# A gated DeltaNet layer with memory cross-attention on one core: side transfers issued by GpSimd, query norms from transposes, output transposes with a shorter gathering time

## The chip, the core and the metric

The kernel runs on one core of a Trainium2 chip. A core has TensorE (PE, the matrix products), VectorE (DVE), ScalarE (ACT), GpSimd (POOL) and SyncE (SP), each with an instruction queue of its own that is worked off in order, and 16 DMA engines that move data between HBM and the on-chip memory SBUF. TensorE writes its results to PSUM, a memory of eight banks, from which VectorE and ScalarE read them. An engine or a queue waits for another through semaphores. The metric is the device time of one execution in microseconds; the time before is 857.72 (median of three runs, 856.27 to 858.84).

## The reference

One layer of a hybrid decoder on 256 tokens of width 2048, all in float32. One wide projection of the normalised input gives all parts; a gated delta rule with 24 value heads (12 query/key heads, two value heads each) and a 4-head softmax cross-attention into 256 memory tokens run side by side; both are gated by SiLU and go through one output projection. Cut to what matters:

```python
h    = rms_norm(x, norm_g)
proj = einsum("bsd,de->bse", h, dn_w_in)                   # 2048 -> 11312 columns
q, k, v, a, b, xq, z = columns of proj
q, k, v = silu(causal_depthwise_conv(q, k, v, width=4))
q = l2_norm(q) * 128**-0.5 ;  k = l2_norm(k)               # per head of 128
g = -exp(a_log) * softplus(a + dt_bias) ;  beta = sigmoid(b)
# S_t = exp(g_t) S_{t-1} (I - beta_t k_t k_t^T) + beta_t v_t k_t^T ;  o_t = S_t q_t
o   = gated_delta_rule(q, k, v, g, beta)                   # chunked, by a triangular solve
mix = rms_norm(o, out_g)                                   # per head of 128
xa  = cross_attention(rms_norm(xq), rms_norm(mem) @ w_kv)  # 4 heads, 256 memory tokens
out = x + (concat(mix, xa) * silu(z)) @ w_out
```

The query's norm is a factor per token and head in front of `o`. Since `o` is normalised afterwards, the kernel doesn't divide the queries: it only needs the sum of the squares of each query, which enters the small constant inside the norm of `o`.

## The kernel before, in words

The weights lie in HBM in tiles of 128 x 1024 and are streamed through SBUF once, in the order of the list `PLAN` (lines 55 to 59): memory values and keys (V, K), gate columns (ab), cross-attention queries (x), keys and queries (k, q), values (v), gates (z), and at the end the output projection (o0 to o3). SP issues every weight load into one of five `st` buffers. For each tile ScalarE makes a rounded copy `hi` (line 342) and VectorE the rest `lo` (line 346) into one of four `wt` buffers; the products are then done as hi·hi + hi·lo + lo·hi with the same split of the activations, which gives float32 accuracy. `proj_a` (lines 362 to 376) makes transposed results (128 features by 256 tokens, PSUM `pa`), `proj_b` (lines 401 to 438) results with tokens in the partitions (`pb`).

Beside this stream run small processes, Python generators, whose instructions are strewn into it: `conv`, `gram` (products of keys, per group of two key heads), `inverse` and `merge` (the triangular inverses of 24 heads in two halves, on VectorE by 32 x 32 blocks, then on TensorE), `v_done` (the convolution of the values: shifted copies made by DMA, taps in `vw`), `delta` (the rule itself, for each of six groups of two key heads and four value heads), `split_y` (transposes of the gated outputs and their split into hi and lo), and `attend` for the cross-attention.

The order is written out by a clock of the program's own. `now` counts the estimated time of TensorE; `ve`, `se` and `po` are the engines' estimated ends; `fin` is the latest estimated end of what the current step has issued. A bare `yield` puts a process to sleep until `fin`. `yield "pe", gather` puts it into a list of those that want TensorE; when the earliest deadline (`now` + gather) is over, all in the list go on together (`step_side`, lines 221 to 228). `pe_soon(GATHER)` is a wait for `fin` plus 1.0 and then such a gathering of 0.5. `until(spare(tag))` waits, by the same clock, for a free PSUM bank; the banks are `pa` 3, `m` 2, `A` 2, `B` 1. `calm` waits until VectorE's estimated backlog is small. None of these waits exists on the chip: there, only the order of instructions and the semaphores of data and buffers count. Up to an estimated time of 45 the order is pinned; behind that, the scheduler of the language may still shift instructions within an engine.

The places that the change touches:

- `Transfers` (lines 128 to 135). `sd.dma_start` raises `fin` by 3.0 and issues from SP. It serves the gates (lines 699, 700, 703), the taps (1173), `gram` (938: two transfers of the Gram matrices to HBM per group), `inverse` (963: two loads `inN`; 989: six loads `n`; 998 and 1000: stores `dY` and `dX`; 1007: four loads into `Y`; 1010: six loads into `XN`; then a wait `LAND` of 9.0 and `merge`) and `v_done` (1182 to 1185: shifted copies `vc`; 1198: four loads `vw`; then a wait `VLAND` of 5.0). The rows of the decay (`erow`, line 734), the weights, the tokens and the results are issued with `sy.dma_start`, SP's own.
- GpSimd otherwise makes the inverse square roots, as a power −0.5 (`rsqrt`, line 270), and memsets.
- `delta` (lines 1243 to 1362). In order: products of keys and queries (`pkq`), `U` of the first block (`pU`, lines 1273 to 1275), its scaled copies, the products across the blocks, `U` of the second block, then the squares of the queries on ScalarE (lines 1324 to 1326, tile `q2` of 2 x 256), then the last products `pO` and, into a bank `m`, the sums of the squares as products with a column of ones (`pqs`, lines 1332 to 1334). Then follow the squares of `o` with an accumulated sum (line 1347), the power `e` on GpSimd and the gating.
- `split_y` (lines 1123 to 1149): for eight pairs of heads it waits for the gated outputs, then `yield "pe", GATHER_Y` with 4.0, then two banks `m`, eight transposes (`pyT`), and the split `yhi`, `ylo`, which the output projection reads.

Of the kernel before, what the change touches and what calls it, by code (L numbers as in the profile page):

```python
# [10 lines left out]
AF = mybir.ActivationFunctionType  # L11
ALU = mybir.AluOpType
# [9 lines left out]
NB = 2  # L22
C = 128
EPS = 1e-6
# [9 lines left out]
LOOK = 2  # L34
WARM = 9
GATHER = 0.5
GATHER_Y = 4.0
XPACE = 3.0
HOP = 0.25
PINNED = 45.0  # L40
# [32 lines left out]
def hybrid_kernel(ctx: ExitStack, tc: tile.TileContext, x, xT, memT, W, prm_d, cst_d, out):  # L73
    nc = tc.nc
    now, fin = [0.0], [0.0]

    def pin(ins):

        return tc.keep_in_program_order(ins) if PINNED is None or now[0] < PINNED else ins
# [8 lines left out]
    te, sy = Pinned(nc.tensor), Pinned(nc.sync)  # L88
# [17 lines left out]
    def width(ap):  # L106
        n = 1
        for d in ap.shape[1:]:
            n *= d
        return n  # L110
# [14 lines left out]
    ve, se = Engine(nc.vector, ve_cost), Engine(nc.scalar, se_cost)  # L125
    po = Engine(nc.gpsimd, lambda e, op, a, k: 0.6)

    class Transfers:


        def dma_start(self, *a, **k):
            fin[0] = max(fin[0], now[0] + 3.0)
            return sy.dma_start(*a, **k)

    sd = Transfers()

# [8 lines left out]
    def S2(name, shape, dt=F32):  # L145
        return s2p.tile([128] + list(shape), dt, name=name, tag="s2")

    def SM(name, shape, bufs=3, dt=F32):
        n = 1
        for d in shape:  # L150
            n *= d
        if n > 128:
            return smp.tile([128] + list(shape), dt, name=name, tag="s1k", bufs=6)
        if n > 16:
            return smp.tile([128] + list(shape), dt, name=name, tag="s512", bufs=3)
        return smp.tile([128] + list(shape), dt, name=name, tag=name, bufs=bufs)

    PB = {"pa": 3, "m": 2, "A": 2, "B": 1}

# [4 lines left out]
    def PS(tag, name):  # L164
        idle[tag].remove(min(idle[tag]))
        pt = ps.tile([128, 512], F32, name=name, tag=tag, bufs=PB[tag])
        held[id(pt)] = (tag, pt)
        return pt

    def spare(tag, n=1):  # L170
        return sum(t <= now[0] for t in idle[tag]) >= n

    def give(pt, t):

        idle[held.pop(id(pt))[0]].append(t)

    def bank(tag, name):
        yield from until(lambda: spare(tag))
        return PS(tag, name)

    def banks(name):
        yield from until(lambda: spare("m", 2))
        return [PS("m", name) for _ in range(2)]
# [10 lines left out]
    def mm(o_, lhsT, rhs, start, stop):  # L194
        n = width(rhs)
        if rhs.dtype == F32:
            now[0] += {32: 0.015, 64: 0.038}.get(rhs.shape[0], max(0.19, 4 * n / 2400.0))
        else:
            now[0] += max(0.092, n / 2400.0 + 0.0137) + 0.01 * (n == 256)
        te.matmul(o_, lhsT, rhs, start=start, stop=stop)  # L200

    def tr(o_, i_):
        now[0] += 0.093
        te.transpose(o_, i_, ident)
# [25 lines left out]
    def until(cond):  # L230
        while not cond():
            yield POLL

    def pe_soon(gather=0.0):

        yield max(fin[0] - now[0], 0.0) + SLACK
        yield "pe", gather
# [9 lines left out]
    def calm(queued=CALM):  # L247

        while ve.end > now[0] + queued:
            yield ve.end - now[0] - queued  # L250
# [5 lines left out]
    ones = cst[:, K_ONE : K_ONE + 1]  # L256
# [144 lines left out]
    def proj_b(steps, act, tag, done, before=None):  # L401
# [4 lines left out]
        for s in range(0, n, 2):  # L406
# [6 lines left out]
            if s == 0 or s + 2 == n:  # L413
                rk.sort()
            if s == 0 and before and tag == "A":

# [463 lines left out]
    KQ = [None] * NPAIR  # L880
# [242 lines left out]
    def split_y():  # L1123
        for j0 in (12, 14, 0, 2, 4, 6, 8, 10):
            jj = (j0, j0 + 1)
            yield from until(lambda: all(yf[j] is not None for j in jj))
            yield from calm(0.8)
            yield "pe", GATHER_Y
            pts = yield from banks("pyT")
# [45 lines left out]
    def v_done(g):  # L1175
# [13 lines left out]
        def done(r, pt):  # L1189
            def go():  # L1190
# [41 lines left out]
                if r == 1:  # L1232
                    vss[g] = raw
                    yield from delta(g)
# [8 lines left out]
    def delta(g):  # L1243

        pp = (2 * g, 2 * g + 1)
# [24 lines left out]
            ve.tensor_tensor(out=kcl[:, i], in0=pkv[i][:, 0:4:2, :], in1=kch[:, i], op=ALU.subtract)  # L1270
            give(pks[i], ve.end)
        yield from pe_soon(GATHER)
        A = yield from bank("A", "pU")
        for w, i, h in heads:
            mm(A[:, w * C : (w + 1) * C], Y[pp[i]][:, 0, h, :], vs[0][:, w, :], start=True, stop=True)
        yield 0.2
        u0s, u0 = S2("u0s", [4, C]), S2("u0", [4, C])
        ve.tensor_tensor(out=u0s, in0=A.rearrange("j (h e) -> j h e", h=4),
                         in1=ekd[:, h4].unsqueeze(2).to_broadcast([128, 4, C]), op=ALU.mult)
        se.copy(u0.rearrange("j h e -> j (h e)"), A)  # L1280
        give(A, max(ve.end, se.end))
        yield
        uh, ul = S2("uh", [4 * C], F32R), S2("ul", [4 * C], F32R)
        u0f = u0s.rearrange("j h e -> j (h e)")
        se.copy(uh, u0f)
        for i, p in enumerate(pp):
            ve.tensor_tensor(out=aT[i], in0=km[:, i].unsqueeze(2).to_broadcast([128, NB, 2, C]), in1=dT[p], op=ALU.mult)
        yield
# [3 lines left out]
        A, B = PS("A", "pU"), PS("B", "pO")  # L1292
# [19 lines left out]
        A, B = PS("A", "pU"), PS("A", "pO")  # L1312
# [8 lines left out]
        for w in range(4):  # L1321
            se.activation(oq[:, w, :], B[:, w * C : (w + 1) * C], AF.Copy, scale=egc[:, 4 * g + w : 4 * g + w + 1])
        give(B, se.end)
        q2 = S2("q2", [2, 256])
        for i, p in enumerate(pp):
            se.activation(q2[:, i, :], KQ[p][:, 1, :], AF.Square)
        yield from pe_soon(GATHER)
        yield from until(lambda: spare("B") and spare("m"))
        B, pq = PS("B", "pO"), PS("m", "pqs")
        for w, i, h in heads:  # L1330
            mm(B[:, w * C : (w + 1) * C], aT[i][:, 1, h, :], u1[:, w, :], start=True, stop=True)
        for b in range(NB):
            for i in range(2):
                mm(pq[:, 2 * b + i : 2 * b + i + 1], q2[:, i, b * C : (b + 1) * C], ones, start=True, stop=True)
        yield 0.2
        ve.tensor_tensor(out=o[1], in0=B.rearrange("c (h e) -> c h e", h=4), in1=oq, op=ALU.add)
        give(B, ve.end)

        eq, e4 = SM("eq", [4], 2), SM("e4", [3, NB, 4], 2)
        ve.tensor_scalar(out=eq, in0=pq[:, 0:4], scalar1=EPS, scalar2=EPS * 128, op0=ALU.add, op1=ALU.mult)  # L1340
        give(pq, ve.end)
        ready.add(f"d{g}")
        yield
        for b in range(NB):
            for w in range(4):
                junk = SM("ojunk", [C])
# [161 lines left out]
```

## Time and profile before

| what | value |
|---|---|
| median of 3 runs | 857.72 us (856.27 to 858.84) |
| the profiled execution | 857.04 us, of which the span of its instructions 855.3 us |
| granted TensorE clock | 1.00 |
| HBM read, written | 167.58 MB, 6.89 MB (204 GB/s over the span) |
| packets of SP's DMA queue | 145080, 180.47 MB |
| DMA issues from GpSimd | none |

A profile has one line per group of instructions: line of the code, engine, operation, the tiles as out<-in, shapes, count; then the time in which at least one of them ran, the mean length of one in ns, and the idle time of the engine before them with what ended it. The lines L86 and L103 are helpers that record every instruction, so groups are told apart by their tiles. Records of TensorE overlap, because products are pipelined and their ends are modelled: the distance from start to start says what a product costs. A float32 product that is not split makes two records, a transpose one.

### The profile page before, as it was taken

The numbers are of one execution on the slowest core, as the hardware profiler recorded it, in microseconds if no ns is written. First come the engines' busy times: TensorE is split into PE (matmuls) and PEld (weight loads), VectorE is DVE, ScalarE is ACT, GpSimd is POOL, SyncE is SP. The second block draws the span as 40 slices with busy tenths as digits, with TensorE's granted clock in tenths as the row PEclk, the third lists the DMA queues.
The fourth block names the chain that finished last, engine by engine and source line by source line (L and its number), as shares of the span: only waits on it lengthen the run. The fifth ranks groups of instructions, "written<-read, shape, count | busy, mean of one in ns | idle before, by whom it ended". The sixth has DMA issues, their size and how long they took to land.

```text
span 855.3 us, 13175 instructions
## 1 busy us (share of the span) xinstructions
PE 848.0 (99%) x4790; PEld 709.7 (83%) x4790; DVE 618.1 (72%) x1080; ACT 538.1 (63%) x929; POOL 46.5 (5%) x45
## 2 busy tenths in 40 slices
PE   9999999999999999999999999999999999999998
PEld 6888888888888888888888888788888888888886
DVE  6878886657779974788889989568886655454442
ACT  7656665798644765995966676679775654333331
POOL 1000000000000000001100202000010000000000
PEclk9999999999999999999999999999999999999999
DMA  9965566448677886869877769686755547666650
GB/s 344 335 218 177 171 189 165 146 147 263 197 208 241 263 243 180 261 210 266 226 243 218 227 214 279 198 242 222 227 158 169 186 142 265 214 210 205 199 197 25
DMA packets 145433, 181.59 MB, mean 212 GB/s; under 512 B 24824, under 2 KB 115824, under 8 KB 145368
## 3 DMA queue, kind: packets, MB, share of 16 engines
q1 hardware_dynamic: 145080, 180.47, 67.0%
q8 instruction: 37, 0.61, 0.3%
q10 hardware_dynamic: 288, 0.28, 0.1%
q14 instruction: 28, 0.23, 0.1%
HBM read 167.58 MB, written 6.89 MB: 204 GB/s over the span
## 4 chain that ended last, share of the span: by engine, by line
PE 95%; ACT 2%; DMA 1%; DVE 1%; issue 1%; SPq 0%; DVEq 0%
PE pb L86 72%; PE pa L86 13%; PE pO L86 2%; PE pU L86 2%; PE pm L86 1%; PE pkq L86 1%; PE pyT L86 1%; ACT dec L103 1%; DVE wt L346 1%; PE pqs L86 1%; PE pkk L86 1%; DMA erow<-dgc 0%; DMA st<-W_d 0%; ACT L103 0%; PE pab L86 0%
## 5 line engine op out<-in xcount | busy, mean ns | idle before, releaser
L346 DVE TENSOR_TENSOR wt<-st,wt 128x1024 fp32r<-128x1024 f32 (+1 forms) x275 | 331.9, 1212 | 164.9 <-ACT wt L342 161.2
L342 ACT CAST wt<-st 128x1024 fp32r<-128x1024 f32 (+1 forms) x275 | 286.3, 1045 | 224.3 <-PE pb L86 180.6
L86 PE MATMUL pb<-wt,hkt 128*128 128x512 f32 x1536 | 361.8, 392 | 0.0
L86 PEld LDWEIGHTS pb<-wt,hkt 128*128 128x128 f32 x1536 | 284.7, 188 | 58.7 <-DVE wt L346 0.4
L86 PE MATMUL pb<-wt,yhi 128*128 128x512 f32 x512 | 158.0, 390 | 0.0
L86 PE MATMUL pa<-hkt,wt 128*128 128x512 f32 (+1 forms) x768 | 142.8, 342 | 0.4 <-DVE wt L346 0.3
L86 PEld LDWEIGHTS pa<-hkt,wt 128*128 128x128 f32 x768 | 117.9, 188 | 18.3 <-DVE wt L346 1.0
L86 PEld LDWEIGHTS pb<-wt,yhi 128*128 128x128 f32 x512 | 95.7, 188 | 19.6
L86 PE MATMUL pb<-wt,ylo 128*128 128x512 f32 x256 | 99.7, 389 | 0.0
L86 PE MATMUL pb<-wt,mkt 128*128 128x512 f32 x384 | 88.6, 391 | 0.9 <-ACT wt L342 0.9
L86 PEld LDWEIGHTS pb<-wt,mkt 128*128 128x128 f32 x384 | 71.6, 188 | 16.8 <-ACT wt L342 1.8
L86 PEld LDWEIGHTS pb<-wt,ylo 128*128 128x128 f32 x256 | 48.1, 188 | 10.1
L103 ACT ACT_TABLE_LOAD x31 | 39.8, 1283 | 1.4 <-DVE acc L103 1.0
L103 DVE SCALAR_TENSOR_TENSOR acc<-raw,prm,acc 128x255 f32<-128x255 f32 (+2 forms) x72 | 34.2, 476 | 3.6 <-ACT acc L103 3.2
L103 DVE TENSOR_TENSOR inT<-inXT,inN 96x1 f32<-96x1 f32 (+22 forms) x92 | 29.1, 342 | 3.2 <-DMA inN<-dN 2.4
L103 DVE TENSOR_REDUCE inXT<-inT 96x1 f32<-96x1 f32 (+22 forms) x92 | 28.6, 337 | 0.7
L103 POOL TENSOR_TENSOR e<-e,mhalf 128x8 f32<-128x8 f32 x6 | 20.8, 3472 | 120.5 <-DVE e L103 120.5
L103 DVE TENSOR_TENSOR vc<-vc 128x512 f32<-128x512 f32 x36 | 24.5, 682 | 0.1
L103 POOL TENSOR_TENSOR srk<-skt,mhalf 128x4 f32<-128x4 f32 x6 | 7.0, 1175 | 224.6 <-DVE skt L103 145.6
L103 DVE SCALAR_TENSOR_TENSOR o<-o,e,zs 128x128 f32<-128x128 f32 x48 | 14.0, 345 | 7.0 <-POOL e L103 7.0
L103 ACT ACTIVATE ojunk<-o 128x128 f32<-128x128 f32 x48 | 14.4, 301 | 7.0 <-DVE o L103 4.9
L103 DVE TENSOR_TENSOR vc<-vc,vw 128x512 f32<-128x512 f32 x24 | 16.4, 683 | 2.8 <-DMA vc<-vs 2.8
(202 smaller groups left out, 693.9 us busy)
## 6 DMA issues: line engine op xcount, KB each, us to landing
st<-W_d SPq DMA_DIRECT2D x271, 512.0 KB
erow<-dgc SPq DMA_DIRECT2D x24, 256.0 KB
vw<-dtap SPq DMA_DIRECT2D x24, 256.0 KB
dN<-dec SPq DMA_DIRECT2D x12, 256.0 KB
n<-dN SPq DMA_DIRECT2D x12, 256.0 KB
vc<-vs SPq DMA_DIRECT2D x12, 224.0 KB
vc<-vc SPq DMA_DIRECT2D x12, 224.0 KB
xraw<-xT_d SPq DMA_DIRECT2D x8, 256.0 KB
```

Of the source, the lines that this page charges most:

```text
L86: return lambda *a, **k: pin(getattr(self.eng, op)(*a, **k))
L103: return pin(getattr(self.eng, op)(*a, **k))
L342: pin(se.eng.copy(hi[:, w] if parts > 1 else hi, st[:, w] if parts > 1 else src))
L346: pin(ve.eng.tensor_tensor(out=lo[:, w] if parts > 1 else lo, in0=st[:, w] if parts > 1 else src, in1=hi[:, w] if parts > 1 else hi, op=AL ...
```

## The change

Three things:

1. `sd.dma_start` issues from GpSimd's queue, no longer from SP's. What raises `fin` stays.
2. In `delta`, the four products with a column of ones go, and so do the two squares of 128 x 256 in front of them. In their place, behind the first `pU` products, four transposes bring the queries to the form tokens by features in a bank `m` (`pqT`), and four squares of 128 x 128 on ScalarE, each with an accumulated sum, give `q2` (128 x 4) directly in SBUF. The wait for a spare bank `m` moves with them.
3. `GATHER_Y` goes from 4.0 to 0.5.

```diff
-GATHER_Y = 4.0
+GATHER_Y = 0.5
...
         def dma_start(self, *a, **k):
             fin[0] = max(fin[0], now[0] + 3.0)
-            return sy.dma_start(*a, **k)
+            return pin(nc.gpsimd.dma_start(*a, **k))
...
         yield from pe_soon(GATHER)
-        A = yield from bank("A", "pU")
+        yield from until(lambda: spare("A") and spare("m"))
+        A, pq = PS("A", "pU"), PS("m", "pqT")
         for w, i, h in heads:
             mm(A[:, w * C : (w + 1) * C], Y[pp[i]][:, 0, h, :], vs[0][:, w, :], start=True, stop=True)
+        for w in range(4):
+
+            tr(pq[:, w * C : (w + 1) * C], KQ[pp[w % 2]][:, 1, w // 2 * C : (w // 2 + 1) * C])
         yield 0.2
...
         se.copy(uh, u0f)
+        q2 = SM("q2", [4], 2)
+        for w in range(4):
+            junk = SM("ojunk", [C])
+            se.activation(junk, pq[:, w * C : (w + 1) * C], AF.Square, accum_out=q2[:, w : w + 1])
+        give(pq, se.end)
...
-        q2 = S2("q2", [2, 256])
-        for i, p in enumerate(pp):
-            se.activation(q2[:, i, :], KQ[p][:, 1, :], AF.Square)
         yield from pe_soon(GATHER)
-        yield from until(lambda: spare("B") and spare("m"))
-        B, pq = PS("B", "pO"), PS("m", "pqs")
+        yield from until(lambda: spare("B"))
+        B = PS("B", "pO")
         for w, i, h in heads:
             mm(B[:, w * C : (w + 1) * C], aT[i][:, 1, h, :], u1[:, w, :], start=True, stop=True)
-        for b in range(NB):
-            for i in range(2):
-                mm(pq[:, 2 * b + i : 2 * b + i + 1], q2[:, i, b * C : (b + 1) * C], ones, start=True, stop=True)
...
-        ve.tensor_scalar(out=eq, in0=pq[:, 0:4], scalar1=EPS, scalar2=EPS * 128, op0=ALU.add, op1=ALU.mult)
-        give(pq, ve.end)
+        ve.tensor_scalar(out=eq, in0=q2, scalar1=EPS, scalar2=EPS * 128, op0=ALU.add, op1=ALU.mult)
```

## Prediction

> **What bounds the kernel now.** I read the page of the profile first: busy times, then the chain that ended last, then the costliest groups.
>
> ```profile
> span 855.3 us, 13175 instructions
> PE 848.0 (99%) x4790; PEld 709.7 (83%) x4790; DVE 618.1 (72%) x1080; ACT 538.1 (63%) x929; POOL 46.5 (5%) x45
> ...
> PE 95%; ACT 2%; DMA 1%; DVE 1%; issue 1%; SPq 0%; DVEq 0%
> ...
> L342 ACT CAST wt<-st 128x1024 fp32r<-128x1024 f32 (+1 forms) x275 | 286.3, 1045 | 224.3 <-PE pb L86 180.6
> ```
>
> PE is busy for 848.0 of 855.3 us and carries 95% of the chain. The third line gives the direction of the waiting: ScalarE, which casts each weight tile, stood idle 224.3 us before that cast, 180.6 of it until PE had given a buffer back. The feed waits for PE, not the reverse. Next, everything PE itself waited for (the view of waits, PE alone: microseconds in total, times, longest), and two lines of the same view for the transfers.
>
> ```profile
> PE warm L86 <- DVE warm L103: 1.2, 1, 1.2
> PE pm L86 <- issue: 1.0, 2, 0.8
> PE pb L86 <- ACT wt L342: 0.9, 1, 0.9
> PE pa L86 <- DVE wt L346: 0.3, 1, 0.3
> ```
>
> ```profile
> ACT wt L342 <- DMA st<-W_d: 3.5, 4, 1.7
> ```
>
> ```profile
> SPq L86 <- DVE wt L346: 368.2, 168, 6.6
> ```
>
> All waits of PE come to 3.4 us, and 2.1 of these (warm and the first weights) are the start. So an edit gains here only by taking instructions off PE; freeing a queue can win back at most the 1.3 us left, plus bubbles too short for this view. SP's queue spends 368.2 us waiting for VectorE to free a weight tile, but late weights held the cast for 3.5 us in all: SP is full of waits that nobody downstream feels. Conversely, any new wait that reaches PE costs its full length.
>
> **The change part by part.** The profiled execution took 857.04 us (span 855.3); the median shown is 857.72, that is 0.68 more. I sum against 857.04 and add the 0.68 at the end.
>
> *Query norms.* Removed per group of two pairs: four fp32 products of 128 rows by one column, `pqs`. Added: four transposes behind the group's first `pU` block. The timeline of PE (start, length, out<-in, count) has all the shapes needed:
>
> ```profile
> 633.22 1.06 PE L86 MATMUL pO<-u,aT 128*128 128x128 f32 x8
> 634.03 5.74 PE L86 MATMUL pb<-wt,hkt 128*128 128x512 f32 x24
> 639.61 1.03 PE L86 MATMUL pyT<-cst,o 128*128 128x128 f32 x8
> 640.48 1.06 PE L86 MATMUL pU<-vc,Y 128*128 128x128 f32 x8
> ...
> 647.55 1.05 PE L86 MATMUL pO<-u,aT 128*128 128x128 f32 x8
> 648.44 0.95 PE L86 MATMUL pqs<-cst,q 128*128 128x1 f32 x8
> 649.26 2.34 PE L86 MATMUL pb<-wt,hkt 128*128 128x512 f32 x9
> ```
>
> Ends are modelled, so I use starts. Four `pO` products (eight records: an fp32 product is two, a transpose one) followed by weights take 634.03 − 633.22 = 0.81 us. The same four followed by `pqs` take until 649.26: 1.71 us. So `pqs` costs 0.90 us a group, though its products are one column wide. Eight transposes in front of `pU` take 640.48 − 639.61 = 0.87, or 0.109 each; four cost 0.44. Saved: 0.46 a group, and with six groups 2.8 us; I take 2.7, since the hundredths are rounded. The transposes join an fp32 block that stands there anyway, so no new change between fp32 and weights is needed.
>
> ScalarE's side, from the tiles `q` and `o` (min/median/max ns):
>
> ```profile
> L103 ACT ACTIVATE q<-kq x12: 429/436/456, 405.7 to 685.1; 128x256 f32<-128x256 f32 x12
> ```
>
> ```profile
> L103 ACT ACTIVATE ojunk<-o x48: 293/298/362, 400.7 to 694.1; 128x128 f32<-128x128 f32 x48
> L103 ACT ACTIVATION_READ_ACCUMULATOR ojunk<-o x48: 185/188/242, 400.9 to 694.3; 128x1 f32 x48
> ```
>
> Removed are 12 x 0.436 = 5.2 us; added are 24 squares of the shape of `ojunk`, with their accumulator reads 24 x 0.486 = 11.7 us if nothing overlaps. ScalarE gains at most 6.5 us, 1.1 per group. Queued behind a square that waits for its transpose are weight casts; PE waits for these only once its buffers run out. I cost it at 0: the 180.6 us in which casts wait for PE hide it. With that cover gone it would be up to 6.5. The wait for a spare `m` bank moves from the group's end to its start; it is settled while the order is written out, and delays the group's chain, not PE. Between −0.5 (the last step gets shorter) and +0.5, I take 0.
>
> *Outputs' transposes.* `GATHER_Y` from 4.0 to 0.5 lets up to eight blocks of eight transposes be placed up to 3.5 us earlier. The danger is PE reaching them before their input. The last ones in the trace:
>
> ```profile
> L103 DVE SCALAR_TENSOR_TENSOR o<-o,e,zs x48: 339/344/353, 418.1 to 702.0; 128x128 f32<-128x128 f32 x48
> ```
>
> ```profile
> 711.94 0.87 PE pyT L86 x8
> 712.81 138.75 PE pb L86 x612
> ```
>
> (The second fence is the chain's end.) The last gating product starts at 702.0 and the transposes at about 711.9, some 9.6 us behind: 3.5 less is still safe. And 612 weight products follow without a hole, so earlier outputs feed nobody who waited. Gain 0. A possible loss: a block that used to lean on another fp32 block now stands alone. The first weight product behind a block costs about 0.1 more (the 24 at 634.03 take 5.58 to 639.61, 0.2325 each, against 138.75/612 = 0.2267), so eight lost neighbours cost 0.8 at worst, three or four likelier: 0.3, inside my rounding.
>
> *Side transfers.* By the code 144 transfers leave SP: 3 for the gates, 1 for the taps, 12 of Gram matrices, 2 x 22 around the inverse, 6 x 14 for the values' shifts. SP's weight loads pass them; by the 3.5 us above that is worth nothing. They now stand in GpSimd's queue, among its powers and memsets, and a transfer that waits for data holds those behind it. For instance VectorE's products `o` wait for GpSimd's power `e`, and weight subtractions queue behind `o`. What a transfer costs there, no row shows. From below: SP's issue, 0.5 us. From above: GpSimd's own slowest small instruction.
>
> ```profile
> L103 POOL TENSOR_TENSOR srk<-skt,mhalf x6: 1006/1006/1912, 191.0 to 394.9; 128x4 f32<-128x4 f32 x6
> ```
>
> ```profile
> L103 POOL TENSOR_TENSOR e<-e,mhalf x6: 1635/3123/6492, 415.1 to 694.9; 128x8 f32<-128x8 f32 x6
> ```
>
> I take 1.0 us, the median of the four-column power, since that too is a small step of fixed cost on this engine; ends 0.5 and 6.5. The tightest place is the merge behind each inverse, where ten transfers follow one another and PE reads what they bring:
>
> ```profile
> 530.25 5.21 SPq L86 DMA_DIRECT2D Y<-dY  x4
> 535.51 3.11 SPq L86 DMA_DIRECT2D XN<-dX  x6
> ```
>
> ```profile
> 548.75 0.26 PE L86 MATMUL pm<-Am,XN 32*32 32x32 f32 x8
> ```
>
> ```profile
> 238.60 1.40 SPq L86 DMA_DIRECT2D dN<-dec  x2
> ...
> 242.38 3.94 SPq L86 DMA_DIRECT2D inN<-dN  x2
> ```
>
> PE reads `XN` 18.5 us after the first of the ten is issued. A transfer lands about 2.4 us after its issue (`inN` could start at 242.38 for a store issued by 240.00). With cost c each, the ten are there after 10c + 2.4: at c = 1.0 that is 12.4, six before PE's need. So 0, hidden by this distance, up to c = 1.6.
>
> *Sum.* 857.04 − 2.7 (products) + 0 + 0 + 0 = 854.3; on the median's footing 855.0. With the profiles' small terms (−1.3 from PE's remaining waits, +0.5, +0.8) this case spans 853.7 to 856.3.
>
> **The rivals.** *A, slower: the merge waits for GpSimd's queue.* If c is above 1.6, PE stands in front of `XN` in both merges, and as its queue is in order, nothing else runs. Time: 857.72 − 2.7 + 2(10c − 16.1). The gain is eaten at c = 1.75; at c = 2.15 the time is 865.8; at 3.1, the middle of `e`, 884.8. For it: `Y` and `XN` go in short pieces of 32 columns, and even SP needed 5.21 us for four. Against it: the whole wait of SP ahead of each transfer (the 6.6 at worst above) goes, so the ten may start earlier.
>
> A rule bears on c, and speaks against this change. The Trainium skill (SBUF — State Buffer, section "SBUF: two separate sides") says that descriptors of GpSimd's transfers are written by its own cores, which VectorE's copies in a two-port mode lock out, and that a transfer of about 620 ns then took about 3100. By that price the estimate would be some 885. How far the trace bears it out:
>
> ```profile
> L103 DVE COPY inN<-inXT 96x256 f32<-96x256 f32 x8 | 3.0, 389 | 0.0
> ```
>
> ```profile
> 540.00:560.00 20.00, 18.95 (x387) 14.87 (x387) 8.06 (x11) 14.35 (x32) 1.03 (x2) 1.00 0.60 209
> ```
>
> SBUF copies of size are eight of 0.39 us, and during the merge VectorE is busy 8.06 of 20 us; so lockout alone should reach few transfers, and A hangs mostly on what a transfer costs by itself. Chance of A: 0.30.
>
> *B, no change that can be measured: the 2.7 us comes back in small coin.* A new order of PE's instructions shifts which block meets which; powers on GpSimd stand behind transfers, and a group's chain gets 1 to 2 us later. For it: VectorE is busy 19.5 of 20 us just before the merge, by the neighbouring window, so a late power is not caught up at once.
>
> ```profile
> 520.00:540.00 20.00, 20.00 (x106) 16.67 (x104) 19.50 (x39) 13.74 (x29) 5.29 (x2) 1.00 0.83 223
> ```
>
> Against it: PE shows no hole there (20.00 of 20). Time: 856 to 858. Chance 0.14.
>
> *C, more than summed: queues come free.* PE's waits in the merge vanish (18.95 of 20 us above: 1.05), and short bubbles with them, one to two us beyond the forecast's edge: 852 to 853.7. Against it: 0.8 of that 1.05 is put down to issue, which no transfer changes. Chance 0.16.
>
> **How the numbers follow.** A measurement here can tell 0.3%, 2.6 us, from no change; the forecast's −2.7 lies just beyond, so it holds both. Forecast 0.40 (0.26 faster, 0.14 the same), C 0.16 (faster), B 0.14 (same), A 0.30 (slower): faster 0.42, same 0.28, slower 0.30. The time is the forecast's, 855.0. The range runs from 852.3 (most of C) to 866, which takes A up to c = 2.15, more than half of it; about 0.18 is left out, nearly all above. The forecast's own range is 853.7 to 856.3.
>
> **What would show it.** Right: `pqs` gone, 24 more transposes of 0.109 us on PE, PE's waits still under 4 us, GpSimd's transfers near 1 us each, and `XN` landed before PE's first `pm<-Am,XN`. Wrong: PE idle in a merge with a transfer as releaser (A); VectorE waiting for `vw` or `vc` and the casts' 180.6 us of waiting for PE shrunk, which would mean that the feed has become the bound; or ScalarE's squares standing between PE and a cast.

## The result and the profile after

The kernel after takes 867.12 us (median of 4 runs, 863.60 to 867.18), the kernel before in the same comparison 857.52: ratio 1.0107, interval 1.0089 to 1.0124. It is slower by 9.6 us, and above the predicted range. Times here and below are of executions with a granted clock of 0.99 or more; the one other, of e11_order, took 1422.59 us at a clock of 0.556.

The page of the kernel after: span and busy times, the chain, the weight cast, and the transfers with their median time from issue to landing.

```profile
span 865.3 us, 13241 instructions
PE 848.9 (98%) x4766; PEld 710.0 (82%) x4766; DVE 619.2 (72%) x1080; ACT 545.6 (63%) x969; POOL 128.9 (15%) x189
...
PE 85%; issue 5%; ACT 4%; DMA 4%; DVE 2%; POOL 0%; SPq 0%; DVEq 0%; ACTq 0%; POOLq 0%
...
L342 ACT CAST wt<-st 128x1024 fp32r<-128x1024 f32 (+1 forms) x275 | 285.8, 1044 | 203.7 <-PE pb L86 175.1
...
st<-W_d SPq DMA_DIRECT2D x271, 512.0 KB, 4.4
erow<-dgc SPq DMA_DIRECT2D x24, 256.0 KB, 5.7
vw<-dtap POOLq DMA_DIRECT2D x24, 256.0 KB, 6.6
```

The sums hardly differ from before: the casts still wait for PE, 175.1 us against 180.6. But PE now carries 85% of the chain instead of 95%. What PE waited for:

```profile
PE pO L86 <- ACT u L103: 6.6, 2, 6.3
PE pm L86 <- issue: 1.3, 1, 1.3
PE warm L86 <- DVE warm L103: 1.2, 1, 1.2
PE pm L86 <- DMA Y<-dY: 1.2, 1, 1.2
```

One wait of 6.3 us is new, and it is for ScalarE. The chain of waits, and ScalarE's timeline at the same place (start, length, what; idle before and its releaser in brackets):

```profile
387.69 12.56 DMA erow<-dgc
...
406.49 0.57 ACT u L103
407.07 0.04 issue
407.11 2.07 PE pO L86 x8
```

```profile
386.90 0.58 ACT L103 COPY vs<-pb 128x512 f32<-128x512 f32 x1
400.36 0.69 ACT L103 ACTIVATE dec<-erow,gcc 128x128 f32<-128x128 f32 x2 [12.89 <-DMA erow<-dgc]
```

In the kernel before, ScalarE came from a weight cast to the same `dec` without a wait:

```profile
398.12 1.05 ACT L342 CAST wt<-st 128x1024 fp32r<-128x1024 f32 x1 [3.34 <-PE pa L86]
399.07 0.69 ACT L103 ACTIVATE dec<-erow,gcc 128x128 f32<-128x128 f32 x2
```

In the kernel after, the row transfer `erow`, on SP's queue, lands 12.56 us after its issue. ScalarE works in order, and its next instruction is `dec`, which reads that row: it stands idle for 12.89 us, with weight casts and the copy `u` behind it. PE runs through its weights and then has nothing. Cut into stretches of 3.4 us, with the granted clock in the third column from the right:

```profile
398.20:401.60 3.40, 2.63 (x16) 2.02 (x14) 0.00 (x0) 1.24 (x4) 0.08 (x1) 1.00 0.95 352
401.60:405.00 3.40, 0.00 (x0) 0.00 (x0) 1.83 (x2) 3.40 (x9) 0.00 (x0) 1.00 0.06 23
405.00:408.40 3.40, 1.29 (x6) 1.29 (x7) 2.78 (x6) 3.40 (x13) 2.14 (x3) 0.50 0.74 228
408.40:411.90 3.50, 3.50 (x12) 2.92 (x12) 3.50 (x6) 2.57 (x5) 3.13 (x6) 0.51 0.58 103
411.90:415.30 3.40, 3.40 (x17) 2.80 (x16) 3.40 (x7) 1.68 (x3) 0.98 (x4) 1.00 0.92 264
```

PE's clock halves at 405.0 us, inside the wait, and is at half for two stretches, 4.8 us of which are work (407.1 to 411.9). So the stall is paid twice: 6.3 us as idle time, and some 2.4 us as work at half speed.

A table for the rest of the document, worked out from the start times in the traces: each instruction of PE is given the median distance to the next start that its tile and shape have in the kernel before (transposes `pqT` 0.109 us). Their sum is PE's own work; what a stretch of the span takes beyond that is its loss (us). Each row is one execution. The rows from e1_norms on are the runs of the next section.

```
                own work   0-385  385-420  420-535  535-575  575-end
before             843.1     4.0      0.1      0.4      2.4      0.3
after              840.3     3.8      8.7      0.2      6.2      0.9
e1_norms           840.3     4.0      3.1      0.3      8.5      0.9
e2_gather          843.1     5.5      0.1      0.3      4.1      0.2
e3_queue           843.1     3.6      8.2      0.0      1.7      0.2
e4_no_queue        840.3     5.9      2.7      0.8      8.3      1.9
e5_lead            843.1     4.8      3.7     -0.1      0.0      5.8
e7_vsp             843.1     3.0      1.4      1.0      1.5      0.2
e8_late            840.3     5.7      2.7      0.8      8.1      0.6
e9_latenorm        840.3     3.6      1.9      0.4      7.6      2.0
e10_after_vsp      840.3     3.0     -0.1      2.4     10.0      0.9
e11_order          843.1     5.8      0.0     -0.1      0.0      9.1
e12_mended         840.3     4.8      0.5      0.2      5.0      0.4
e13_fix_before     843.1    14.2      2.6      6.1      3.8      6.2
e14_fix_queue      843.1    10.2      9.1      3.5      8.0      6.2
e15_fix_vsp        843.1    13.0      5.6      4.9      6.7      6.3
e16_fix_order      843.1    11.1      4.4      1.0      3.7     14.1
```

After against before: own work −2.8, 385 to 420 us +8.6, 535 to 575 us (the second merge) +3.8, the rest +0.2; together +9.8, where the two profiled spans differ by 10.0. The saving is there, and two places of 35 and 40 us eat four times as much.

### The profile page after: what moved, and what is told of

The parts are those of the page before. It is cut to its first block, busy times and chain, and to the rows that moved or that the text cites. A ratio compares the mean times of both kernels' runs of the same rounds, so it can differ in the third digit from the quotient of the medians.

```text
span 865.3 us, 13241 instructions
## 1 busy us (share of the span) xinstructions
PE 848.9 (98%) x4766; PEld 710.0 (82%) x4766; DVE 619.2 (72%) x1080; ACT 545.6 (63%) x969; POOL 128.9 (15%) x189
## 4 chain that ended last, share of the span: by engine, by line
PE 85%; issue 5%; ACT 4%; DMA 4%; DVE 2%; POOL 0%; SPq 0%; DVEq 0%; ACTq 0%; POOLq 0%
PE pb L86 67%; PE pa L86 10%; DMA erow<-dgc 3%; PE pO L86 2%; PE pU L86 1%; DVE wt L346 1%; ACT dec L103 1%; PE pkq L86 1%; PE pyT L86 1%; ACT wt L342 1%; ACT L103 1%; PE pm L86 1%; DMA st<-W_d 0%; PE pab L86 0%; PE xo L86 0%
## 5 line engine op out<-in xcount | busy, mean ns | idle before, releaser
L342 ACT CAST wt<-st 128x1024 fp32r<-128x1024 f32 (+1 forms) x275 | 285.8, 1044 | 203.7 <-PE pb L86 175.1
L86 PEld LDWEIGHTS pb<-wt,ylo 128*128 128x128 f32 x256 | 48.0, 188 | 10.3 <-DVE ylo L103 0.4
L103 ACT ACTIVATE dec<-erow,gcc 128x128 f32<-128x128 f32 x48 | 16.5, 396 | 20.8 <-DMA erow<-dgc 20.8
L133 POOL DMA_DIRECT2D vc<-vc x30 | 15.8, 531 | 64.9 <-DVE vc L103 45.9
L103 POOL TENSOR_TENSOR e<-e,mhalf 128x8 f32<-128x8 f32 x6 | 11.0, 1836 | 92.6 <-DVE e L103 92.6
L133 POOL DMA_DIRECT2D vc<-vs x30 | 16.0, 539 | 30.2 <-ACT vs L103 18.0
```

What stands on the lines that cost most here:

```text
L86: return lambda *a, **k: pin(getattr(self.eng, op)(*a, **k))
L103: return pin(getattr(self.eng, op)(*a, **k))
L133: return pin(nc.gpsimd.dma_start(*a, **k))
L342: pin(se.eng.copy(hi[:, w] if parts > 1 else hi, st[:, w] if parts > 1 else src))
```

## The experiments

Ratios are to the kernel before, run beside each group on the same chip.

**The parts alone.** Each of the first four undoes parts of the change. e1_norms has the new norms and the rest as before; e2_gather the 0.5 alone; e3_queue the queue alone; e4_no_queue all but the queue.

```
e1:  after, but  GATHER_Y = 4.0  and  return sy.dma_start(*a, **k)
e2:  before, but GATHER_Y = 0.5
e3:  before, but return pin(nc.gpsimd.dma_start(*a, **k))
e4:  after, but  return sy.dma_start(*a, **k)
```

> The kernel before with the query norms alone changed (transposes and accumulating squares); side transfers stay on SP, GATHER_Y stays 4.0. Theory Q (all of the loss comes from GpSimd's queue; the norms gain what was summed): 2.7 us less than before, some 854.8, with no wait of PE above 1.5 us. Rival N (ScalarE's added squares hold a copy that PE waits for): not faster, 857 to 862, and the view of waits shows PE waiting for ACT.

Measured: 864.39 us, ratio 1.0080 (1.0059 to 1.0100).

> The kernel before with GATHER_Y at 0.5 alone. Theory Q: no change, 857 to 858. Rival G (earlier output transposes disturb the order on ScalarE and VectorE): slower by 1 us or more.

Measured: 857.84 us, ratio 1.0001 (0.9988 to 1.0013).

> The kernel before with the side transfers alone moved to GpSimd's queue. Theory Q: the whole loss and none of the gain, 867 + 2.7, some 870; a wait of ScalarE for erow of several us and slow landings stay. If the loss needs the three edits together (rival S, an accident of the new order of instructions): nearer to 857 to 860.

Measured: 865.31 us, ratio 1.0092 (1.0070 to 1.0114).

> The changed kernel with its side transfers given back to SP: norms and GATHER_Y alone. Theory Q: 854.8 (2.7 below before), PE's waits under 4 us as before. Rival S: still above 860.

Measured: 865.81 us, ratio 1.0088 (1.0072 to 1.0105).

Theory Q falls. The norms alone lose 6.4 us though PE has 2.8 us less to do, the queue alone loses 7.3, and both together only 9.6. `GATHER_Y` is worth nothing, as forecast. By the table the queue loses at 385 to 420 us, and there alone. The two kernels with the new norms and no change of the queue (e1_norms, e4_no_queue) lose most at the second merge, 8.5 and 8.3 us, and some 3 us at 385 to 420 us, where in e1_norms ScalarE waits 2.5 us for a weight tile. The norms' stall at the merge, in the chain of e1_norms:

```profile
549.56 0.91 PE pO L86 x8
...
550.56 0.70 DVE o L103
551.26 0.02 issue
551.28 1.29 ACT ojunk L103 x8
...
552.94 1.62 POOL e L103
...
555.46 1.15 DVE wt L346
556.60 0.04 issue
556.65 0.79 PE pb L86
```

The end of group 2 (the third of six, since they are counted from 0: last products, squares of `o`, GpSimd's power `e`, gating `o`) has slid into the merge, and on VectorE it stands ahead of the weight subtraction that PE waits for. In the kernel before that same power began at 530.7, ahead of the merge. PE is idle for 2.4 us, and then its clock is at half for 10.2. From this came theory P, named in the next expectations: the loss is made at two thin places, by one engine that stands in order behind something late, and the half clock adds to it.

**Four attempts on the mechanism.** Three change e3_queue and one e1_norms:

```
 e5  -        yield 3.0                         (decay, behind its first load of erow)
     +        yield 3.0 if rows else 9.0
 e6  +        if g == 0:                        (in delta, ahead of the last pO)
     +            for _ in range(12):
     +                te.matmul(B, warm[:, 0:128], warm, start=True, stop=True)
 e7  -        sd.dma_start(dst...), sd.dma_start(w[j]...)    (v_done: vc, vw)
     +        the same on SP, by sy.dma_start, fin raised by 3.0 as before
 e8  +        yield 6.0                         (in delta, ahead of the gating products)
```

> Transfers on GpSimd's queue alone, as in e3_queue (865.3 us), and beside it the second pause of the decay step is 9.0 instead of 3.0 in the order's own time, so that ScalarE's dec stands later among the weight casts. Theory P (thin places: ScalarE, in order, stands behind a transfer that lands late, PE runs dry for about 2.5 us near 400 us, and the granted clock then halves for 10 us): the stall at 400 us and the half clock after it are gone, what PE loses between 385 and 420 us falls from 8.2 us to under 1, and the time is 857 to 858.5. Rival Q (GpSimd's queue costs its time everywhere, whatever ScalarE's order): 864 to 866, as e3_queue. If the erow transfer is simply met later by the next thing in ScalarE's order: 862 to 866 with the stall some us later.

Measured: 864.96 us, ratio 1.0079 (1.0063 to 1.0095). Missed. The stall at 401 us shrinks to 1.4 us of idle time and the half clock to 3.4 us, but the later decay moves the second merge from 546 us in e3_queue to 585, and behind 575 us this kernel loses 5.8 us, e3_queue 0.2.

> As e3_queue (865.3 us), and 12 needless bf16 products of 128x128 by 512 columns go to PE right before group 0's pO products, where it ran dry at 401.8 us for 2.76. The result of the kernel is not changed; PE has about 2.6 us more work by 0.22 us each. Theory P (most of the price is the half clock that follows the idle time): PE is busy through the wait, the clock stays at 1.0 between 400 and 416 us, and the kernel with MORE work is faster than e3_queue by some 4 to 5 us: 860 to 861.5. If the wait alone is the price and the clock is only a sign of it: 865 to 868, no faster than e3_queue.

Measured: 863.76 us, ratio 1.0070 (1.0050 to 1.0090). Where the products were added, theory P holds:

```profile
400.00:404.00 4.00, 2.93 (x12) 1.37 (x13) 2.76 (x4) 4.00 (x15) 1.35 (x3) 1.00 0.32 94
404.00:408.00 4.00, 3.83 (x25) 2.85 (x23) 4.00 (x7) 4.00 (x10) 4.00 (x7) 1.00 0.87 194
```

The clock stays at 1.00, and the stretch 385 to 420 us loses 4.9 us instead of 8.2, although 2.7 of the 4.9 are the 12 needless products. More work there made this stretch faster by 3.3. But this kernel lost 5.0 at the merge, where e3_queue lost 1.7, so that the whole gained only 1.6.

> As e3_queue (865.3 us), but the transfers of the values' shifts (vw and vc, 84 of the 144) stay in SP's queue; the other 60 go over GpSimd's. If erow lands 12 us after its issue because the shifts of group 1 take half of the DMA engines' time from a second queue: erow lands in under 8 us, ScalarE's dec waits for it under 4 us, no stall at 400 us, and 857 to 858.5. If any of GpSimd's other transfers, or its own work, is the cause: 863 to 866 with the stall where it was.

Measured: 858.16 us, ratio 1.0008 (0.9992 to 1.0024). With 84 of the 144 transfers back on SP the loss of the queue is gone. Its chain, and ScalarE ahead of the same `dec`:

```profile
389.08 7.04 DMA erow<-dgc
```

```profile
389.99 1.05 ACT L346 CAST wt<-st 128x1024 fp32r<-128x1024 f32 x1 [3.78 <-PE pa L86]
392.76 1.05 ACT L346 CAST wt<-st 128x1024 fp32r<-128x1024 f32 x1 [1.73 <-PE pa L86]
396.15 0.70 ACT L103 ACTIVATE dec<-erow,gcc 128x128 f32<-128x128 f32 x2 [2.34 <-DMA erow<-dgc]
```

Two things differ from e3_queue at once: `erow` lands after 7.0 us instead of 11.8, and ScalarE has two casts ahead of `dec` that it did not have there, because the scheduler orders each engine anew when the transfers stand elsewhere. This run doesn't say which of the two counts.

> Norms alone as in e1_norms (864.4 us), and a pause of 6.0 in the order's own time before VectorE's gating products, so that they stand behind more weight subtractions. Theory P (at the second merge VectorE's gating products wait for GpSimd's power e, a weight subtraction stands behind them, PE runs dry 2.5 us at 554 us and the clock halves): the loss between 535 and 575 us falls from 8.5 us to about 2.4, as in the kernel before; the stall at 403 us stays (2 to 4 us); the time is 857.5 to 860. If the norms' early squares or transposes hold PE by themselves wherever the gating stands: 863 to 866.

Measured: 862.34 us, ratio 1.0046 (1.0030 to 1.0062). Mostly missed: 8.1 us are still lost at the merge, by another chain. GpSimd's power `e`, begun at 541.49, took 8.36 us there, and products, copies and a cast queued behind it in turn.

**Place, order or form?** e9_latenorm leaves the new norms at the place where `pqs` was; e10_after_vsp is the kernel after with the shifts on SP as in e7_vsp; e11_order is the kernel before with the one pause of e5_lead; e12_mended is the whole change with the norms of e9_latenorm and the shifts on SP.

```
 e9  -        B, pq = PS("B", "pO"), PS("m", "pqs")
     +        B, pq = PS("B", "pO"), PS("m", "pqT")
     ...      (pO products)
     -        four products pqs of q2 with ones
     +        for w in range(4): tr(pq[...], KQ[...]);  then four se.activation(..., AF.Square, accum_out=...)
 e11 -        yield 3.0
     +        yield 3.0 if rows else 9.0
```

> Norms alone in the change's form (four transposes into a bank of m, four accumulating squares, no pqs products), but at the old place: behind the group's last pO products, where the kernel before had pqs, so that no group waits for a spare bank of m at its start. PE's own work is as in e1_norms, 2.8 us less than before. Theory M (in e1_norms the wait for a bank of m at the group's start puts group 2's chain behind the second inverse, its end into the merge; the form itself is good): no stall at 554 us and no half clock there, 854.5 to 857. Rival F (the squares on ScalarE hold a copy that PE waits for, wherever they stand): 861 to 866. Rival S (any new order of the instructions loses some us at the thin places): 858 to 864.

Measured: 863.01 us, ratio 1.0061 (1.0047 to 1.0075). Theory M falls: without any wait for a bank at the group's start the merge still loses 7.6 us. There PE now waits 2.0 us for ScalarE's copies `Y`, which stand in order behind `vc`, `dec`, squares of `o` and two loads of a function table (ACT_TABLE_LOAD), 1.28 us each, of which the kernel before has one there. Rivals F and S both forecast this time. But no new square is seen at the place: in all seven kernels with the new norms none starts between 532 and 594 us. So F doesn't explain the merge directly, for there is no new square there that could hold a copy.

> The kernel after (867.1 us), but the values' shifts (84 transfers) stay in SP's queue. Theory P with e7_vsp: the stall at 400 us and its half clock go (8.7 us of loss there to about 1.5), the loss in the merge that comes with the early norms stays: 858.5 to 862. If the two parts lose in one shared way, and not each at its own place: 865 to 867.

Measured: 861.80 us, ratio 1.0052 (1.0034 to 1.0071). As theory P has it: the loss at 385 to 420 us goes from 8.7 to nothing, the merge keeps its own and even loses 10.0 (one wait of 5.2 us for ScalarE's `Am`, in a chain that goes back to a shift `vc` on SP's queue that took 11.94 us to land).

> The kernel before with one pause of the decay step at 9.0 instead of 3.0, all transfers on SP, the old norms: a change of the written order and of nothing else, the same one as in e5_lead. It measures what an arbitrary change of the order costs. Rival S (the tuned order is the point, and any change of it loses): 860 to 866. If the order alone is harmless, and the queue and the early norms do the harm: 857 to 859.

Measured: 864.80 us, ratio 1.0081 (1.0066 to 1.0096). No transfer, no norm, no instruction of PE was changed, only one pause in the written order, and it costs 7.5 us. The second merge lies at 582 us now and loses 9.1. The chain there:

```profile
576.35 7.20 DMA st<-W_d
...
584.38 1.61 PE pm L86 x113
585.99 3.14 issue
589.13 0.43 PE pm L86 x11
```

So a loss of this size needs neither part of the change; a new order alone can make it.

> The whole change with two corrections: norms at the old place as in e9_latenorm, the values' shifts on SP as in e7_vsp, the other 60 transfers on GpSimd, the outputs' transposes at 0.5. If both causes are right and no third one is left: 854.5 to 857.5, faster than both kernels. If the parts disturb each other by their order: 859 to 864.

Measured: 855.79 us, ratio 0.9976 (0.9963 to 0.9989): faster than before by 0.24%, some 2 us, and by 11 than the change as made; below the 0.3% that one measurement tells, but the interval excludes no change. Its profiled execution took 858.46 us and was the slowest of its twelve, so its row in the table stands on the high side: the stall at 400 us is gone there too, the merge's is not.

**The same order, with and without the queue.** With `PINNED = None` instead of 45.0 all instructions stay in the order in which the program writes them, and nothing is shifted behind it. Then the queue can be changed without changing any order: e14_fix_queue has the instructions of e13_fix_before on PE, ScalarE and VectorE, one for one. e15_fix_vsp is e14_fix_queue with the shifts on SP, e16_fix_order is e13_fix_before with the pause of e11_order. The new norms were not tried in this way.

```
-PINNED = 45.0
+PINNED = None
```

> The kernel before with PINNED at None: every instruction is kept in the order in which the kernel's own planner writes it, where otherwise only the planner's first 45 us are kept and the compiler's scheduler orders the rest. By itself it measures what the scheduler's order is worth: 857 to 870. It is the base for the two that follow, whose PE, ScalarE and VectorE have exactly its order.

Measured: 886.29 us, ratio 1.0339 (1.0317 to 1.0361). The scheduler's order is worth 29 us.

> e13_fix_before with the side transfers on GpSimd's queue: PE, ScalarE and VectorE have the same instructions in the same order, so that only the queue differs. Theory H (the queue itself does the harm: two queues share the DMA engines and everything lands late): 5 to 9 us above e13_fix_before, with the loss near 400 us. Theory O (the harm of e3_queue is the new order that the scheduler makes once the transfers stand on another engine): within 2 us of e13_fix_before.

Measured: 887.19 us, ratio 1.0339 (1.0319 to 1.0359), the same ratio as e13_fix_before. In the whole, theory O is right; but the stretch shows that the queue does some harm by itself. The windows 385 to 420 us of e13_fix_before, then of e14_fix_queue:

```profile
385.00:420.00 35.00, 33.80 (x186) 28.62 (x186) 28.16 (x59) 17.91 (x34) 4.28 (x8) 0.98 0.75 215
```

```profile
385.00:420.00 35.00, 29.28 (x157) 24.56 (x156) 24.92 (x56) 16.96 (x31) 17.54 (x28) 0.90 0.72 214
```

In the same order PE does 157 products instead of 186 there, at a lower clock, and loses 6.5 us more; `erow` and the weight tiles issued at that time land after 11.6 to 13.2 us. The `erow` that ScalarE's `dec` waits for takes 12.4 us here, and 6.4 in e13_fix_before (issued at 400.80, read at 407.17). At the merge it loses 4.2 more, of which PE waits 3.2 for `Y`: rival A's wait, here in one merge. It loses 4.0 less ahead of 385 us and 2.6 less between 420 and 535, where this slower kernel has losses to win back. (The sum, +4.1, is that of the two profiled executions; that of e13_fix_before was the fastest of its five, 3.4 under its median, so the medians differ by 0.9 only.)

> e14_fix_queue with the values' shifts back on SP, again the same order on PE, ScalarE and VectorE. Theory H: within 2 us of e13_fix_before, as e7_vsp was of the kernel before. Theory O: the same as both, and nothing is told apart.

Measured: 886.61 us, ratio 1.0335 (1.0320 to 1.0349). The totals tell nothing apart. In the stretch, the same `erow` is read 6.8 us after its issue again, and the loss at 385 to 420 us is 5.6, between the 9.1 of e14_fix_queue and the 2.6 of e13_fix_before: in these executions about half of the harm comes with the shifts, and what makes the other half isn't known.

> e13_fix_before with the decay's second pause at 9.0 instead of 3.0, as e11_order is to the kernel before (there +7.8 us): a change of the planner's order alone, with no scheduler behind it. If any shift of the second inverse's place costs some 8 us: 6 to 10 us above e13_fix_before. If it was the scheduler's answer to the shift that cost it: within 3 us.

Measured: 886.43 us, ratio 1.0333 (1.0313 to 1.0353). The pause that cost 7.5 us under the scheduler costs nothing here in the whole. By the table, though, it loses 7.9 us more than e13_fix_before behind 575 us, where the second merge now lies, as e11_order lost 8.8 more than the kernel before; and it wins 8.2 back ahead of 385 and between 420 and 535 us, where the fixed order has losses to win back. So the total doesn't show that the merge's new place is harmless.

What is settled: under the scheduler the queue's loss at 400 us goes when the shifts go back to SP (8.2 to 1.4 us in e7_vsp, 8.7 to nothing in e10_after_vsp), and with the order held fixed the shifts on the second queue still make `erow` land late (12.4 us against 6.4 and 6.8) and cost time there. What stays open: how much of the 7 us of e3_queue is landing and how much the new order, and why all seven kernels with the new norms lose 5 us or more at the merge. That group 2 begins 5 to 15 us later in them (its first `pU` at 501 to 511 us, before at 496) and so runs into the merge, is seen in their traces; what sets it back is not. Nor is the late end enough by itself: in e3_queue the power `e` of that group begins at 547.2 us, inside the merge, and only 1.7 us are lost there.

## Why the prediction was wrong, step by step

*What bounds the kernel.* Right, and it held: PE does the same work in sequence, and each new wait that reached it cost its full length. What was missed is that a wait costs more than its length, since the clock halves behind it. No term of the sum had the clock; the profile before showed it at 1.00 throughout, and so gave no price.

*Query norms on PE.* Right: −2.8 us by start times, −2.7 forecast. The view of the tile in the kernel after has the 24 transposes, and ScalarE's squares at the size taken for them:

```profile
L86 PE MATMUL pqT<-cst,kq x24: 272/273/273, 375.1 to 686.9; 128*128 128x128 f32 x24
L103 ACT ACTIVATE ojunk<-pqT x24: 255/278/298, 376.1 to 688.0; 128x128 f32<-128x128 f32 x24
```

ScalarE's busy time grew by 7.5 us in the kernel after, a little more than the 6.5 taken as the most. Of these, 5.1 are four more loads of function tables, which e3_queue has too and e1_norms has not: they come with the queue's new order.

*What the norms do to the order, "delays the group's chain, not PE" and "I cost it at 0".* This step failed: the term for all that is not PE's own work, put at 0 within 0.5 on either side. The norms' part of the change as a whole cost 6.4 us (e1_norms) instead of −2.7. By the table 6.1 us more than before were lost at the second merge and 3.0 at 385 to 420 us. At the merge the group's delayed chain did reach PE: its power `e` began at 552.9 us instead of 530.7, and its gating came to stand ahead of weights. The wait for a spare bank, of which the first quoted words speak, isn't the whole cause: in e9_latenorm, without it, the merge lost 7.6 us all the same. The cover, "the 180.6 us in which casts wait for PE hide it", is a sum over the whole span and says nothing of stretches where there is no such cover. The added squares, which it was to hide, aren't what PE waited for at the merge: none of them lies there. Why the group begins later, and why the merge loses in each of the seven kernels, stays open; that a new order alone can cost as much, e11_order shows with 7.5 us.

*Outputs' transposes.* Right: 0 forecast, ratio 1.0001 measured.

*Side transfers, the cost on GpSimd's queue.* The term was right. GpSimd's own rows (busy, mean ns):

```profile
L133 POOL DMA_DIRECT2D vw<-dtap x24 | 18.1, 761 | 13.2 <-DVE inXT L103 10.1 <-DVE vc L103 3.0
L133 POOL DMA_DIRECT2D XN<-dX x12 | 7.3, 618 | 10.5 <-DMA dX<-inN 10.5
L133 POOL DMA_DIRECT2D Y<-dY x8 | 5.8, 726 | 4.3 <-issue 4.2
```

By these rows and the others of that view between 0.5 and 1.0 us each, c below the 1.6 from which rival A was to decide; PE waited 1.2 us for `Y` in one merge and never for `XN`. Rival A, whose range reached the right times, named the wrong place and the wrong transfers. The Trainium skill's price of about 3100 ns (SBUF — State Buffer, section "SBUF: two separate sides") is seen nowhere: no transfer on GpSimd's queue has a mean above 1.01 us, with VectorE busy 72% of the span. Only 17 of its 1080 instructions are copies (4.7 us), of which the skill speaks, so this case hardly tests that price.

*Side transfers, the landing.* "A transfer lands about 2.4 us after its issue" failed, and with it "SP's weight loads pass them; by the 3.5 us above that is worth nothing". In the kernel after the median is 4.4 us for weight tiles, 5.7 for `erow` and 6.6 for `vw`, and it is 12.6 for the `erow` that is under way together with the shifts and the weights. The 2.4 came from one store; the chain of the kernel before already had an `erow` of 4.27 us (from 169.64). Between 388 and 400 us the profile gives the DMA engines a busy share of 0.92 to 1.08 in the kernel after, and of 0.83 to 1.06 in the kernel before (4 us at a time): they are about full in both, and what changed is what was under way together. The late transfer that cost time was not one of those that moved but an `erow`, which stayed on SP's queue, and the place was the start of the values' shifts, not the merge. The Trainium skill says it (DMA: Bandwidth & Descriptors, section "Issuing engines are not separate DMA queues"): transfers from all issuing engines run on the same 16 DMA engines and interleave, and a second issuer saves only the time of issuing. The traces agree, with `erow` at 12.56 us beside shifts from the second queue and at 7.04 in e7_vsp, where SP issues the shifts itself; it is the rule that should have been weighed here.

*Rival B.* Of all that was written down it comes nearest to the norms' loss ("a new order of PE's instructions shifts which block meets which"), but at 2.7 us. Measured are 4.5 to 7.5 us above the kernel before, in e8_late, e9_latenorm and e11_order.

## What to carry to other kernels

A sum of waiting time over the whole span covers nothing by itself: look for the stretches in which the feed is not ahead, and ask of each edit what it puts there ahead of a weight on an engine that works in order. Where a scheduler orders the instructions, every edit is also a new order; so measure the edit's parts, and one change of order that does nothing else, before a cause is believed. Moving transfers to an idle engine's queue moves the issuing and not the engines that carry the bytes.

## What the runs showed of the hardware

**The clock halves for steps of 3.41 us, and can do so on less than 3.41 us of idle time.** In the traces of all these kernels the half clock, where it comes within the work, lasts 3.41, 6.83 or 10.24 us, and all its edges in one trace lie whole multiples of 3.41 us apart. The Trainium skill (TensorE: Matmul & The Clock Gate, section "Part 1: The HAM clock gate") has a free-running window of 3413 ns, which agrees, and half the clock after at least one idle window. The kernel after has such a window (401.60 to 405.00 us, no product), but the half clock also came without one. In e2_gather (first pair) and e8_late (two pairs), each pair is such a window and the next one:

```profile
555.80:559.20 3.40, 2.66 (x59) 2.06 (x59) 1.23 (x1) 2.41 (x4) 0.51 (x1) 1.00 0.03 5
559.20:562.60 3.40, 3.40 (x46) 2.73 (x43) 1.22 (x1) 3.40 (x10) 0.00 (x0) 0.50 0.72 202
```

```profile
406.10:409.50 3.40, 1.56 (x11) 1.48 (x12) 2.06 (x4) 3.12 (x9) 0.00 (x0) 1.00 1.04 298
409.50:412.90 3.40, 3.40 (x17) 2.81 (x16) 3.40 (x6) 3.29 (x6) 0.00 (x0) 1.00 0.95 179
...
556.30:559.70 3.40, 1.09 (x54) 0.66 (x44) 0.80 (x1) 3.38 (x8) 0.00 (x0) 1.00 0.15 48
559.70:563.10 3.40, 2.92 (x8) 1.83 (x9) 0.47 (x2) 3.29 (x8) 0.52 (x1) 0.50 0.46 129
```

0.74 us of idle time among the merge's products of 64 x 64 halved the clock; 1.84 us among weight and `pO` products did not; 2.31 in a merge did again. So the kind of work in the window may count beside the idle time; but among weight products alone both happen too, since in e13_fix_before the window from 355.4 us, with 1.8 us idle among them, was followed by the half clock. Laid on this grid, every window at full clock with more than 1.84 us idle was followed by the half clock in these traces (between the first 5 us and 850 us); between 0.74 and 1.84 us some were and some weren't, and what decides there these runs don't show. Since the windows run freely, the same gap can fall into one window or be shared by two, which may be why one kernel, e8_late, was measured between 858.7 and 865.4 us; that is argued and not shown.

**GpSimd's small power can stretch beside VectorE, its transfers don't.** The power `e` takes 1.64 us at its shortest and 11.81 at its longest, by the tile's row in e8_late:

```profile
L103 POOL TENSOR_TENSOR e<-e,mhalf x6: 1636/1795/11807, 417.6 to 702.2; 128x8 f32<-128x8 f32 x6
```

In the longest, from 470.96 us, VectorE works without a break for 10.3 us and then rests for 1.5, in which the power ends. In all these traces every power above 2.1 us has VectorE busy for at least 59% of its time, and most of those at 1.64 us have it idle. But a busy VectorE isn't enough: in e12_mended the power at 612.2 us took 1.64 with VectorE busy throughout. The transfers on GpSimd's queue had no such tail: in the kernel after none took more than 1.04 us.
